# Attention without transposed probabilities: second scores with the keys on the partitions

## The chip, the core and the metric

The kernel runs on one core of a Trainium2 chip. The metric is the device time of one execution in microseconds (us), here as the median of the runs. The core has five engines with a queue each: TensorE (PE) multiplies matrices out of SBUF into PSUM, its weight loads are shown apart as PEld; VectorE (DVE) and ScalarE (ACT) work elementwise and read and write PSUM; GpSimd (POOL) works elementwise in SBUF and issues some of the DMAs; SyncE (SP) issues most DMAs. Each engine executes its queue in order.

## The reference

One layer of a hybrid diffusion backbone over 512 latent tokens and 256 context tokens, width 1024: a modulated RMS norm, one input projection, a bidirectional state-space mixer beside windowed attention, gated merge and output projection, then a gated convolutional feed-forward part. The change concerns the attention of the latent queries:

```
s_win  = q . k * scale          (latent keys within +-128, masked by -inf outside)
s_ctx  = q . k_ctx * scale      (all 256 context keys)
logits = concat(s_win, s_ctx, sink)      16 heads, 4 key heads, head size 64
p      = softmax(logits)
o      = p[window] @ v + p[context] @ v_ctx
```

Queries are taken in blocks of 128. A block sees its own, the block before and the block after (those that exist) and two context blocks: 4 or 5 key blocks of 128.

## The kernel before

All large products are done in fp32r, with each fp32 operand split into a high part (rounded by ACT) and a low part (the difference, by DVE). A product of a 128 x 128 weight block with 512 columns is three matmuls: high by high, high by low, low by high (`gemm`, L232 to L241).

The attention stage handles 16 blocks `n`: key head `j = n // 4` with its four query heads, query block `b = n % 4`. `block_atoms` (L956) lists the steps of a block as atoms: a name, an engine, a planned duration, the atoms it needs, a rank, and the function that emits it. `Plan.order` (L342) goes through them as a small planner: on each engine the atom of lowest rank that is ready next is taken, and its planned end releases others. The result is one fixed order by hand for the engines named in `manual_schedule` (L1383). Beside the blocks the plan holds products from the list `BESIDE` (L1364; `product_atoms`, L1085): the query projections of later heads, the second key projection, and gate and output projections, in pieces of three matmuls. Their matmuls have the highest rank numbers, so TensorE takes them when no attention step is ready; their weight splits (`w`, `v`) and evacuations come first on ACT and DVE.

A block before the change, with c = 4 or 5 key blocks:

- `score(i)`: per head, queries on the partitions. A query tile holds the high part in one half of the 128 rows and the low part in the other; the keys' high parts (`khi`, in both halves) and low parts (`klo`) are multiplied one after the other, into one score tile of 512 or 640 keys.
- `least(i)` on DVE adds the window mask and takes the negated maximum over keys and sink into a column of `mneg`; `exps(i)` on ACT makes the exponentials and their sum; `sink`, `sum_` and `norm(i)` divide them.
- `turn(x, i)` transposes each head's 128 x 128 probabilities of key block x by TensorE into a PSUM bank; `high(x)` and `low(x)` split the result; `values(x, y)` multiplies each part with a 128-wide stationary operand whose columns are the values' high (64) and low (64) parts. `out_low` and `out_sum` add the two halves of the result into `att`.

`q_high` and `q_low` (L899, L904) split a projected pair of query heads and place the parts in the halves of two tiles by three DMAs on SP. `k_high`, `k_low`, `k_double` do the like for the keys. `v_step` (L917) projects the values just before the stage and splits them. `split_atoms` (L1345) splits `att` for the output projection and reuses the tiles of the keys. `sum_step` (L160) issues the weight-sum DMAs of the feed-forward part on POOL, each behind one of the products' DVE splits (32 in this stage, one or two per product).

Of the kernel before, what the change touches and what calls it, by code (L numbers as in the profile page):

```python
# [44 lines left out]
def tile_hybrid_layer(  # L45
# [25 lines left out]
    win_d: bass.AP,  # L71
    fg_d: bass.AP,
# [178 lines left out]
    dtv = cpool.tile([P, 2], F32, name="dtv")  # L251
    sel = cpool.tile([P, P], U8, name="sel")
# [166 lines left out]
    winm = ap.tile([P, 896], F32, name="winm")  # L419

# [6 lines left out]
    with tc.tile_pool(name="spool", bufs=1) as sp:  # L427
# [69 lines left out]
        def load_tables():  # L497
            nc.sync.dma_start(vec[:, V_N2:], vecs[:, V_N2:])
            self_ = raws["self"] = sp.tile([P, P], F32, name="self_")
            nc.sync.dma_start(self_, sel_d)  # L500
            for d, s in ((cosb, cos_d), (sinb, sin_d), (winm, win_d), (bcs, bc.partition_broadcast(P)), (dtv, dta)):
                nc.sync.dma_start(d, s)
# [333 lines left out]
    khi = attp.tile([P, 4, 768], F32R, name="khi")  # L836
    klo = attp.tile([P, 4, 768], F32R, name="klo")

    kt = [k.rearrange("p a b -> p (a b)")[:, i * L : (i + 1) * L] for k in (khi, klo) for i in range(6)]
    atth, attl = kt[0:4] + [None] * 2 + kt[4:6], kt[6:10] + [None] * 2 + kt[10:12]  # L840
    vst = a2p.tile([P, 6, 4, P], F32R, name="vst")
# [22 lines left out]
    def k_high(r, t, z):  # L864

        S.copy(khi[:, 2 * t, z], r[:, : z.stop - z.start])

    def k_low(r, t, z):
        V.tensor_tensor(klo[:, 2 * t, z], r[:, : z.stop - z.start], raw(khi[:, 2 * t, z]), ALU.subtract)
# [10 lines left out]
    def k_step(t):  # L880
        def fn(w, r=None):
            if r is None:
                pl = accb()
                gemm([LAT(pl)], w)
                r = rope(pl, -0.125)
            pc = accb()
            gemm([CTX(pc)], w)
            rc = tmp("tc")
            S.activation(rc[:, :LC], pc[:, :LC], AF.Copy, scale=-0.125)
            for x, z in ((r, KL), (rc, KC)):  # L890
                k_high(x, t, z)
                k_low(x, t, z)
            k_double(t)

        return [("k", t)], fn
# [3 lines left out]
    def q_high(r, t):  # L899
        q = [attp.tile([P, L], F32R, tag="q", name="q", bufs=7) for _ in range(2)]  # L900
        S.copy(q[0], r)
        Q.update({2 * t: q[0], 2 * t + 1: q[1]})

    def q_low(r, t):  # L904

        q = Q[2 * t], Q[2 * t + 1]
        lo = tmp("tc").bitcast(F32R)
        V.tensor_tensor(lo, r, raw(q[0]), ALU.subtract)
        for o, i in ((q[1][64:128, :], q[0][64:128, :]), (q[1][0:64, :], lo[64:128, :]), (q[0][64:128, :], lo[0:64, :])):
            nc.sync.dma_start(raw(o), raw(i))  # L910
# [6 lines left out]
    def v_step(*w):  # L917
# [32 lines left out]
    psum_pools(acc=(2, 1), score=(1, 2), pt=(3, 1), po=(1, 1))  # L950
# [5 lines left out]
    def block_atoms(n, turned):  # L956
# [5 lines left out]
        cols = parts[0] + parts[1]  # L962
        w, c = len(cols) * P, len(cols)
        o0 = P if w == 640 else 0
        m = winm[:, 0:512] if b == 3 else winm[:, 896 - w :]
        d = {"pt": {}, "pth": {}, "ptl": {}, "p": {}, "ps": {}}
        R = 1000 * n

        def score(i):
            h = 4 * j + i  # L970
            if i == 0:
                d["mneg"] = a2p.tile([P, 4], F32, tag="mneg", name="mneg", bufs=2)
                d["den"] = a2p.tile([P, 4], F32, tag="den", name="den", bufs=2)
            ps = d["ps"][i] = bank("score")
            o = o0
            for z in parts:
                for v, k in enumerate((khi, klo)):
                    T.matmul(  # L978
                        ps[:, o : o + len(z) * P], Q[h][:, b * P : (b + 1) * P], k[:, j, z[0] * P : (z[-1] + 1) * P],
                        start=v == 0 and o % 512 in (0, P), stop=v == 1, skip_group_check=True,  # L980
                    )
                o += len(z) * P

        def least(i):
            h = 4 * j + i
            p = d["p"][i] = a2p.tile([P, 640], F32, tag="p", name="p", bufs=NP_)
            V.tensor_tensor_reduce(  # L987
                p[:, :w], d["ps"][i][:, o0 : o0 + w], m, op0=ALU.add, op1=ALU.min, scale=1.0,
# [3 lines left out]
        def exps(i):  # L992
            p = d["p"][i][:, :w]
            S.activation(p, p, AF.Exp, bias=d["mneg"][:, i : i + 1], scale=-1.0, accum_out=d["den"][:, i : i + 1])  # L994

        def sink():
            d["es"] = a2p.tile([P, 4], F32, tag="es", name="es", bufs=2)
            V.tensor_tensor(d["es"], bcs[:, 32 + 4 * j : 36 + 4 * j], d["mneg"], ALU.add)

        def sum_():  # L1000
            V.tensor_tensor(d["es"], d["es"], d["den"], ALU.add)
            V.reciprocal(d["es"], d["es"])

        def norm(i):
            p, e = d["p"][i][:, :w], d["es"][:, i : i + 1]
            if i % 2:
                S.activation(p, p, AF.Copy, scale=e)
            else:
                V.tensor_scalar(p, p, e, None, ALU.mult)

        def turn(x, i):
            if x not in d["pt"]:
                d["pt"][x] = bank("pt")
            T.transpose(d["pt"][x][:, i * P : (i + 1) * P], d["p"][i][:, x * P : (x + 1) * P], ident)  # L1014

        def high(x):
            d["pth"][x] = a2p.tile([P, L], F32R, tag="pth", name="pth", bufs=2)
            S.copy(d["pth"][x], d["pt"][x])  # L1018

        def low(x):  # L1020
            d["ptl"][x] = a2p.tile([P, L], F32R, tag="ptl", name="ptl", bufs=2)
            V.tensor_tensor(d["ptl"][x], d["pt"][x], raw(d["pth"][x]), ALU.subtract)  # L1022

        def values(x, y):
            if x == 0 and y == "pth":
                d["po"] = bank("po")
            T.matmul(  # L1027
                d["po"], vst[:, cols[x], j, :], d[y][x], start=x == 0 and y == "pth", stop=x == c - 1 and y == "ptl"
            )

        def out_low():
            d["o2"] = tmp("tc")
            S.copy(d["o2"][0:64, :], d["po"][64:128, :])

        def out_sum():
            po4 = d["po"][0:64, :].rearrange("p (t u q) -> p u t q", t=2, u=2)
            o24 = d["o2"][0:64, :].rearrange("p (t u q) -> p u t q", t=2, u=2)
            for u in range(2):
                V.tensor_tensor(
                    att[64 * u : 64 * u + 64, 2 * j : 2 * j + 2, b * P : (b + 1) * P], po4[:, u], o24[:, u], ALU.add  # L1040
                )
            if n == 3:
# [6 lines left out]
        for i in range(4):  # L1049
# [4 lines left out]
            atom("S%d.%d" % (n, i), "PE", 0.83e-3 * w + 0.055, needs, R - 600 + 10 * i, lambda i=i: score(i))  # L1054
            needs = ["S%d.%d" % (n, i)] + (["c%d" % (n - 2)] if n > 1 else [])
            if k >= NP_:
                f, g = of(k, NP_)
                needs.append("T%d.%d.%d" % (f, (3, 4, 4, 3)[f % 4], g))
            atom("r%d.%d" % (n, i), "DVE", 1.09e-3 * w + 0.195, needs, R - 600 + 10 * i, lambda i=i: least(i))
            atom("e%d.%d" % (n, i), "ACT", 0.83e-3 * w + 0.39, ["r%d.%d" % (n, i)], R - 600 + 10 * i, lambda i=i: exps(i))  # L1060
        atom("a%d" % n, "DVE", 0.16, ["r%d.3" % n], R + 50, sink)
        atom("b%d" % n, "ACT", 0.19, ["a%d" % n], R + 50, lambda: S.activation(d["es"], d["es"], AF.Exp))
        atom("c%d" % n, "DVE", 0.37, ["b%d" % n, "e%d.3" % n], R + 50, sum_)
        for i in range(4):
            e, cost = ("ACT", 0.84e-3 * w + 0.28) if i % 2 else ("DVE", 0.52e-3 * w + 0.215)
            atom("n%d.%d" % (n, i), e, cost, ["c%d" % n], R + 60 + i, lambda i=i: norm(i))
        for x in range(c):
            g, nx = len(turned), "%d.%d" % (n, x)
            turned.append(nx)
            for i in range(4):  # L1070
                needs = ["n%d.%d" % (n, i)] + (["l" + turned[g - 3]] if g > 2 else [])
                atom("T%s.%d" % (nx, i), "PE", 0.109, needs, R + 100 + 10 * x + i, lambda x=x, i=i: turn(x, i), load=0.055)
            back = turned[g - 2] if g > 3 else None
            needs = ["T%s.%d" % (nx, i) for i in range(4)]
            atom("h" + nx, "ACT", 0.587, needs + (["H" + back] if back else []), R + 100 + 10 * x, lambda x=x: high(x))
            atom("l" + nx, "DVE", 0.687, ["h" + nx] + (["L" + back] if back else []), R + 100 + 10 * x, lambda x=x: low(x))
            needs = ["h" + nx] + (["H%d.%d" % (n, x - 1)] if x else ["f%d" % (n - 1)] if n else [])
            atom("H" + nx, "PE", 0.227, needs, R + 104 + 10 * x, lambda x=x: values(x, "pth"))
# [1308 lines left out]
```

## Time and profile before

| what | value |
|---|---|
| time, median of 3 runs | 1217.41 us (1216.89 to 1217.82) |
| profiled execution: its span, first to last instruction | 1215.7 us |
| median of the runs less that span | 1.7 us |
| TensorE clock granted | 1.000 |
| attention stage: first score, last value matmul | 94.4 us, 317.4 us |
| transposes of probabilities, start of first and last | 108.5 us, 315.5 us |
| matmuls of scores, transposes, values | 256, 288, 144 |

The profile gives no other time for the profiled execution than its span; the runs that are timed have no profile. In a line of a group stand source line, engine, operation, output and inputs by the program's names, shapes, count, then busy time in us and mean duration in ns, then the engine's idle time ahead of the group and what ended it. In a line of a timeline stand start, duration, engine, line, operation. Matmuls are pipelined, so their durations overlap; the distance from one start to the next tells what a matmul takes of the stream.

### The profile page before, as it was taken

Reading aid. Unit: us, or ns where it says so; the run is one execution under the profiler, and the core shown is the slowest. Engines: PE = TensorE matmul, PEld = TensorE weight load, DVE = VectorE, ACT = ScalarE, POOL = GpSimd, SP = SyncE. Lnnn points to the kernel's source line nnn. Section 1 sums busy time; section 2 is a strip of 40 time slices with the busy share of each in tenths; the row PEclk is TensorE's granted clock in tenths of the full one; section 3 lists DMA queues with packets and bytes.
Section 4 is the critical chain, followed back from the end, with each engine's and each line's share of the span. In section 5 each row is a group of like instructions: output and inputs, shape, how many; then the busy total and the mean of one; then the engine's idle time right before and its main releaser. Section 6 shows DMA issues by size and latency. Waiting matters only on the chain.

```text
span 1215.7 us, 17471 instructions
## 1 busy us (share of the span) xinstructions
PE 1208.4 (99%) x6288; PEld 992.9 (82%) x6288; DVE 923.6 (76%) x1494; ACT 683.4 (56%) x1269; POOL 220.9 (18%) x242
## 2 busy tenths in 40 slices
PE   9999999999999999999999999999999999999998
PEld 6798888888878877778787778888988888888886
DVE  5857888888565688697896867677687777778787
ACT  5557787778544367476575664223543443436654
POOL 0000121100102534252451622000200100110021
PEclk9999999999999999999999999999999999999999
DMA  9655889834758525356366558777266634436662
GB/s 371 258 139 184 160 239 263 170 139 137 170 154 257 172 85 175 116 128 202 96 160 207 171 186 273 242 232 249 51 161 149 194 118 135 133 105 222 214 185 98
DMA packets 124424, 215.74 MB, mean 177 GB/s; under 512 B 26697, under 2 KB 69745, under 8 KB 124337
## 3 DMA queue, kind: packets, MB, share of 16 engines
q1 hardware_dynamic: 110256, 187.09, 49.1%
q0 software_dynamic: 13792, 27.27, 9.9%
q8 instruction: 49, 0.80, 0.3%
q14 instruction: 39, 0.31, 0.1%
q10 hardware_dynamic: 288, 0.27, 0.1%
HBM read 187.78 MB, written 44.89 MB: 191 GB/s over the span
## 4 chain that ended last, share of the span: by engine, by line
PE 98%; issue 1%; DVE 0%; ACT 0%; POOL 0%; DVEq 0%; POOLq 0%; ACTq 0%
PE acc L238 20%; PE acc L241 20%; PE acc L239 20%; PE score L978 3%; PE po L1027 3%; PE pt L1014 2%; PE mis L581 2%; PE mis L1707 2%; PE mis L1579 2%; PE mis L2244 2%; PE mis L2245 2%; PE mis L2243 2%; PE mis L1715 1%; PE acc L2244 1%; PE acc L2245 1%; PE acc L2243 1%
## 5 line engine op out<-in xcount | busy, mean ns | idle before, releaser
L183 ACT CAST whi<-wraw 128x1024 fp32r<-128x1024 f32 (+1 forms) x115 | 120.3, 1047 | 159.3 <-PE acc L239 104.7
L184 DVE TENSOR_TENSOR wlo<-wraw,whi 128x1024 fp32r<-128x1024 f32 (+1 forms) x115 | 144.7, 1259 | 68.2 <-ACT whi L183 65.8
L238 PE MATMUL acc<-hlh,whi 128*128 128x512 f32 x472 | 193.9, 411 | 0.0
L239 PE MATMUL acc<-hll,whi 128*128 128x512 f32 x472 | 184.9, 392 | 0.0
L241 PE MATMUL acc<-hlh,wlo 128*128 128x512 f32 x472 | 184.9, 392 | 0.0
L241 PE MATMUL acc<-mh,wlo 128*128 128x512 f32 x368 | 143.3, 389 | 0.0
L238 PE MATMUL acc<-mh,whi 128*128 128x512 f32 x368 | 143.3, 389 | 0.0
L239 PE MATMUL acc<-ml,whi 128*128 128x512 f32 x368 | 143.2, 389 | 0.0
L241 PEld LDWEIGHTS acc<-hlh,wlo 128*128 128x128 f32 x472 | 88.6, 188 | 19.5
L238 PEld LDWEIGHTS acc<-hlh,whi 128*128 128x128 f32 x472 | 88.8, 188 | 17.9 <-issue 2.8
L239 PEld LDWEIGHTS acc<-hll,whi 128*128 128x128 f32 x472 | 88.9, 188 | 17.4 <-issue 2.4
L241 PEld LDWEIGHTS acc<-mh,wlo 128*128 128x128 f32 x368 | 69.1, 188 | 14.9 <-DVE wlo L184 0.5
L239 PEld LDWEIGHTS acc<-ml,whi 128*128 128x128 f32 x368 | 69.1, 188 | 14.4
L238 PEld LDWEIGHTS acc<-mh,whi 128*128 128x128 f32 x368 | 69.1, 188 | 14.2
L987 DVE CUSTOM_DVE_ANT_0 p<-score,winm,nsink 128x512 f32<-128x512 f32 (+1 forms) x64 | 51.8, 810 | 15.3 <-PE score L978 13.8
L1412 DVE SCALAR_TENSOR_TENSOR ta<-acc,half,ta 128x511 f32<-128x511 f32 (+1 forms) x66 | 43.8, 664 | 23.2 <-ACT ta L1411 23.0
L164 POOL DMA_DIRECT2D dsum<-wdn x24 | 25.4, 1146 | 193.1 <-DVE wlo L1111 171.8
L1411 ACT ACTIVATE ta<-acc,half 128x512 f32<-128x512 f32 (+1 forms) x66 | 46.8, 710 | 24.3 <-PE acc L241 23.0
L994 ACT ACTIVATE p<-p,mneg 128x512 f32<-128x512 f32 (+1 forms) x64 | 49.7, 777 | 15.4 <-DVE mneg L987 14.8
L1022 DVE TENSOR_TENSOR ptl<-pt,pth 128x512 fp32r<-128x512 f32 x72 | 47.5, 685 | 8.7 <-ACT pth L1018 7.7
L238 PE MATMUL acc<-hch,whi 128*128 128x256 f32 x176 | 53.2, 302 | 0.0
L812 DVE SCALAR_TENSOR_TENSOR tm<-wraw,csil,tm 128x512 f32<-128x512 f32 x56 | 43.1, 770 | 12.7 <-DMA wraw<-wm 12.0
(454 smaller groups left out, 3011.1 us busy)
## 6 DMA issues: line engine op xcount, KB each, us to landing
wraw<-wup SPq DMA_DIRECT2D x44, 512.0 KB, 3.8
dsum<-wdn POOLq DMA_DIRECT2D x24, 704.0 KB, 8.7
wraw<-wm SPq DMA_DIRECT2D x32, 512.0 KB, 3.6
fb<-cs_d SPq DMA_DIRECT2D x32, 512.0 KB, 6.6
wraw<-wx SPq DMA_DIRECT2D x24, 512.0 KB, 3.6
wm<-wm SPq DMA_DIRECT2D x16, 512.0 KB, 8.3
wraw<-wz SPq DMA_DIRECT2D x16, 512.0 KB, 4.3
wraw<-wos SPq DMA_DIRECT2D x16, 512.0 KB, 4.7
```

Of the source, the lines that this page charges most:

```text
L183: F["cast"] = S.copy(hi[:, :n], r[:, :n])
L184: F["sub"] = V.tensor_tensor(lo[:, :n], r[:, :n], raw(hi[:, :n]), ALU.subtract)
L238: T.matmul(ps, wh, xh[:, k0 + k, :], start=a, stop=False)
L239: T.matmul(ps, wh, xl[:, k0 + k, :], start=False, stop=False)
L241: T.matmul(ps, wl, xh[:, k0 + k, :], start=False, stop=b)
L812: V.scalar_tensor_tensor(acc, r[:, u * 512 : u * 512 + 512], sc, acc, ALU.mult, ALU.add)
L987: V.tensor_tensor_reduce(p[:, :w], d["ps"][i][:, o0 : o0 + w], m, op0=ALU.add, op1=ALU.min, scale=1.0, scalar=nsink[:, h : h + 1], accum_o ...
L994: S.activation(p, p, AF.Exp, bias=d["mneg"][:, i : i + 1], scale=-1.0, accum_out=d["den"][:, i : i + 1])
L1022: V.tensor_tensor(d["ptl"][x], d["pt"][x], raw(d["pth"][x]), ALU.subtract)
L1411: S.activation(o[:, :n], ps[:, :n], AF.Identity, scale=hcol(base_w, stride + i), bias=hcol(base_b, i))
L1412: x = V.scalar_tensor_tensor(o[:, 1:n], ps[:, 0 : n - 1], hcol(base_w, i), o[:, 1:n], ALU.mult, ALU.add)
L2243: T.matmul(ps, h, wh, start=st, stop=False, skip_group_check=True)
```

## The change

Scores are computed twice. The first time, with queries on the partitions as before, serves the maximum alone, and only the product with the keys' tile `kboth` (high part in rows 0 to 63, low part in rows 64 to 127) by a query tile that has the high part in both halves is taken: one matmul where there were two.

The maxima of a block's four heads are transposed by TensorE to four rows (`turn_shift`), copied by ACT and put by a DMA on ACT's queue as row 64 under the queries' low parts (`row(64)`); a second row, 96, gets the exponential of sink minus maximum (`row(96)`). Row 64 of the key tile `kone` is -1.

The second scores (`turned_score`) have keys on the partitions and 4 heads x 128 queries as columns: one matmul of `kboth` by the queries' high parts, and one of 65 rows, the keys' high parts and the row of -1 by the queries' low parts and the row of maxima. The result is masked on DVE where a key block lies beside the query block, and exponentiated by ACT straight into an SBUF tile `p`. No transposes, no splits of probabilities.

The values are kept in fp32, 64 columns wide. `values(x)` is two fp32 matmuls of 256 columns, one for each pair of heads, into the lower and upper 64 partitions of the result. The denominators: POOL adds the tiles `p` and the sink's row (`add`, `add_sink`), TensorE multiplies the sum with ones (`total`), DVE takes reciprocals and multiplies (`share`, `put`). The plan now orders POOL's instructions of this stage too. The rows of the attention's output projection are reordered on the host to match the new order of heads in `att`. PSUM in this stage: two banks for products, one pair for scores, two for second scores and two for results (before: two, one pair, three for transposes, one). The scratch space for POOL's DMA descriptors is set to 4096 bytes a partition.

```diff
     def k_high(r, t, z):
-        S.copy(khi[:, 2 * t, z], r[:, : z.stop - z.start])
+        S.copy(kboth[:, 2 * t + 1, z], r[:, : z.stop - z.start])
     def k_low(r, t, z):
-        V.tensor_tensor(klo[:, 2 * t, z], ..., raw(khi[:, 2 * t, z]), ALU.subtract)
-    def k_double(t):
-        for k in (khi, klo):
-            for a in (64, 0):
-                nc.sync.dma_start(raw(k[a : a + 64, 2 * t + 1, :]), raw(k[64:128, 2 * t, :]))
-            nc.sync.dma_start(raw(k[64:128, 2 * t, :]), raw(k[0:64, 2 * t, :]))
+        V.tensor_tensor(kone[:, 2 * t + 1, z], ..., raw(kboth[:, 2 * t + 1, z]), ALU.subtract)
+    def k_place(t):
+        h = kboth[:, 2 * t + 1, :], kone[:, 2 * t + 1, :]
+        lo, hi = slice(0, 64), slice(64, P)
+        for o, i in (
+            (kboth[lo, 2 * t, :], h[0][lo]), (kone[lo, 2 * t, :], h[0][lo]), (kboth[hi, 2 * t, :], h[1][lo]),
+            (kboth[lo, 2 * t + 1, :], h[0][hi]), (kone[lo, 2 * t + 1, :], h[0][hi]), (kboth[hi, 2 * t + 1, :], h[1][hi]),
+        ):
+            nc.sync.dma_start(raw(o), raw(i))
+        G.tensor_scalar(kone[64:65, 2 * t : 2 * t + 2, :], ones..., -1.0, None, ALU.mult)
...
     def q_low(r, t):
+        j, i = divmod(2 * t, 4)
+        (b, a), lo, hi = Q[j], slice(0, 64), slice(64, P)
+        V.tensor_tensor(a[:, i, :], r, raw(b[:, i, :]), ALU.subtract)
+        for o, x in (
+            (b[lo, i + 1, :], b[hi, i, :]), (b[hi, i + 1, :], b[hi, i, :]), (a[lo, i + 1, :], a[hi, i, :]),
+            (b[hi, i, :], b[lo, i, :]),
+        ):
+            nc.sync.dma_start(raw(o), raw(x))
...
-            S.copy(vst[:, t, :, 0:64], o)
-            V.tensor_tensor(vst[:, t, :, 64:128], o, raw(vst[:, t, :, 0:64]), ALU.subtract)
+            S.copy(vst[:, t, :, :], o)
...
-    psum_pools(acc=(2, 1), score=(1, 2), pt=(3, 1), po=(1, 1))
+    psum_pools(acc=(2, 1), score=(1, 2), st=(2, 1), po=(2, 1))
...
+        cols = con + [b] + ([b + 1] if b < 3 else []) + ([b - 1] if b else [])
...
+        def turn_shift():
+            d["po"] = bank("po")
+            d["mt"] = d["po"][0:4, 256:384]
+            T.transpose(d["mt"], raw(d["mr"]), ident)
+        def row(part):
+            t = a2p.tile([4, P], F32, tag="row%d" % part, name="row", bufs=2)
+            if part == 64:
+                S.copy(t, d["mt"])
+            else:
+                S.activation(t, d["mt"], AF.Exp, bias=sink4[:, j : j + 1])
+            S.dma_start(raw(Q[j][1][part : part + 1, :, tok]), t)
+        def turned_score(x):
+            ps, k = bank("st"), slice(cols[x] * P, (cols[x] + 1) * P)
+            T.matmul(ps, kboth[:, j, k], Q[j][0][:, :, tok], start=True, stop=False)
+            T.matmul(ps, kone[0:65, j, k], Q[j][1][0:65, :, tok], start=False, stop=True)
+        def exps(x):
+            d["p"][x] = a2p.tile([P, L], F32, tag="p", name="p", bufs=NP_)
+            S.activation(d["p"][x], d["st"][x], AF.Exp, scale=-1.0)
+        def add(x):
+            ...
+                G.tensor_tensor(d["sum"], d["p"][0] if x == 1 else d["sum"], d["p"][x], ALU.add)
+        def add_sink():
+            s = h4(d["sum"])[96:97]
+            G.tensor_tensor(s, s, raw(Q[j][1][96:97, :, tok]), ALU.add)
+        def values(x):
+            for u in range(2):
+                T.matmul(
+                    d["po"][64 * u : 64 * u + 64, 0:256], vst[:, cols[x], j, :], d["p"][x][:, 256 * u : 256 * u + 256],
+                    start=x == 0, stop=x == c - 1, skip_group_check=True,
+                )
+        def total():
+            for u in range(2):
+                T.matmul(
+                    d["po"][64 * u : 64 * u + 64, 256:512], ones[:, 0:64], d["sum"][:, 256 * u : 256 * u + 256],
+                    start=False, stop=True, skip_group_check=True,
+                )
+        def share():
+            V.reciprocal(d["rec"], d["po"][:, 256:512])
+        def put():
+            V.tensor_tensor(att[:, 2 * j : 2 * j + 2, tok], x, r, ALU.mult)
...
+        atom("bt%d" % n, "PE", 0.1, ["bm%d" % n] + (["f%d" % (n - 2)] if n > 1 else []), R - 550, turn_shift, load=0.03)
+        atom("bg%d" % n, "ACT", 0.66, ["bt%d" % n], R - 550, lambda: row(64), whole=False)
+        atom("bM%d" % n, "DMA", 3.0, ["bg%d" % n], R, None)
...
+            needs = ["bM%d" % n] + ([turned[g - 2]] if g > 1 else [])
+            atom("s" + nx, "PE", 0.454, needs, R + 100 + 10 * x, lambda x=x: turned_score(x))
...
+            atom("e" + nx, "ACT", 0.62, needs, R + 100 + 10 * x, lambda x=x: exps(x))
+            needs = ["e" + nx] + (["V%d.%d" % (n, x - 1)] if x else [])
+            atom("V" + nx, "PE", 0.427, needs, R + 104 + 10 * x, lambda x=x: values(x))
...
+            atom("A" + nx, "POOL", 1.4 if x else 0.0, needs, R + 104 + 10 * x, lambda x=x: add(x))
+        atom("bz%d" % n, "POOL", 1.0, ["A%d.%d" % (n, c - 1), "bE%d" % n], R + 170, add_sink)
+        atom("bd%d" % n, "PE", 0.214, ["bz%d" % n, "V%d.%d" % (n, c - 1)], R + 180, total)
+        atom("bc%d" % n, "DVE", 1.9, ["bd%d" % n], R + 180, share)
+        atom("f%d" % n, "DVE", 0.42, ["bc%d" % n], R + 180, put)
...
-    with tc.manual_schedule(engines={mybir.EngineType.PE, mybir.EngineType.Activation, mybir.EngineType.DVE}):
+    with tc.manual_schedule(engines={mybir.EngineType.PE, mybir.EngineType.Activation, mybir.EngineType.DVE, mybir.EngineType.Pool}):
...
-    nc = bacc.Bacc("TRN2", target_bir_lowering=False, num_devices=1)
+    nc = bacc.Bacc("TRN2", target_bir_lowering=False, num_devices=1, dynamic_dma_scratch_size=4096)
```

More of the change, by code (lines that the diff above doesn't have):

```diff
@@ L990, in least @@
             )
[L992 to L1002, printed above, removed]
@@ L1020, in low @@
[L1020 to L1033, printed above, removed]
@@ L1061, in block_atoms @@
[L1061 to L1066, printed above, removed]
+            atom("S%d.%d" % (n, i), "PE", 0.42e-3 * w + 0.027, needs, R - 600 + 10 * i, lambda i=i: score(i))
@@ L1067, in block_atoms @@
+        atom("bM%d" % n, "DMA", 3.0, ["bg%d" % n], R, None)
+        atom("bi%d" % n, "ACT", 0.7, ["bg%d" % n], R - 540, lambda: row(96), whole=False)
+        atom("bE%d" % n, "DMA", 3.0, ["bi%d" % n], R, None)
         for x in range(c):
             g, nx = len(turned), "%d.%d" % (n, x)
[L1069 to L1078, printed above, removed]
@@ L1079, in block_atoms @@
[L1079 to L1083 removed]
+            turned.append("e" + nx)
+            needs = ["bM%d" % n] + ([turned[g - 2]] if g > 1 else [])
```

147 lines of the change are left out of this document (73 added, 74 removed).

## Prediction

> **What bounds the kernel now.** I read the page's head and chain of waits first, then the stretch view of the attention stage, then its instruction groups, then TensorE's timeline inside it.
>
> ```profile
> span 1215.7 us, 17471 instructions
> PE 1208.4 (99%) x6288; PEld 992.9 (82%) x6288; DVE 923.6 (76%) x1494; ACT 683.4 (56%) x1269; POOL 220.9 (18%) x242
> PE 98%; issue 1%; DVE 0%; ACT 0%; POOL 0%; DVEq 0%; POOLq 0%; ACTq 0%
> ...
> 108.00:318.00 210.00, 209.95 (x1166) 179.55 (x1165) 175.25 (x363) 168.05 (x328) 26.60 (x28) 1.00 0.71 185
> ```
>
> The last row's columns are length, then busy time of TensorE (PE), its weight loads, VectorE (DVE), ScalarE (ACT), GpSimd (POOL), then granted clock, DMA share and GB/s. TensorE sets the end and its clock is full. In the attention stage it has no idle time (209.95 of 210.00), while DVE and ACT are at 83% and 80%. "Busy" overlaps between matmuls, so I price TensorE by the distance between starts. Work taken from DVE or ACT gains nothing by itself here; a microsecond taken from or put on TensorE's stream counts in full.
>
> **What goes away.** The stage's groups:
>
> ```profile
> L987 DVE CUSTOM_DVE_ANT_0 p<-score,winm,nsink 128x512 f32<-128x512 f32 (+1 forms) x64 | 51.8, 810 | 15.3 <-PE score L978 13.8 <-PE pt L1014 1.2
> L994 ACT ACTIVATE p<-p,mneg 128x512 f32<-128x512 f32 (+1 forms) x64 | 49.7, 777 | 15.4 <-DVE mneg L987 14.8
> L1022 DVE TENSOR_TENSOR ptl<-pt,pth 128x512 fp32r<-128x512 f32 x72 | 47.5, 685 | 8.7 <-ACT pth L1018 7.7 <-PE po L1027 0.9
> L1014 PE MATMUL pt<-ident,p 128*128 128x128 f32 x288 | 41.7, 272 | 0.0
> L1018 ACT CAST pth<-pt 128x512 fp32r<-128x512 f32 x72 | 40.5, 589 | 9.2 <-PE pt L1014 5.4 <-DVE ptl L1022 2.9
> L1027 PE MATMUL po<-ptl,vst 128*128 128x512 f32 x72 | 28.6, 408 | 0.0
> L1007 ACT ACTIVATE p<-p,es 128x512 f32<-128x512 f32 (+1 forms) x32 | 23.7, 771 | 5.5 <-DVE es L1002 5.4
> L1009 DVE TENSOR_SCALAR p<-p,es 128x512 f32<-128x512 f32 (+1 forms) x32 | 15.5, 521 | 0.2
> ```
>
> and TensorE's timeline (start, duration, line):
>
> ```profile
> 150.87 0.28 PE L978 MATMUL score<-khi,q 128*128 128x256 f32 x1
> ...
> 151.35 0.39 PE L238 MATMUL acc<-hlh,whi 128*128 128x512 f32 x1
> 151.58 0.40 PE L239 MATMUL acc<-hll,whi 128*128 128x512 f32 x1
> ...
> 152.97 0.34 PE L978 MATMUL score<-khi,q 128*128 128x384 f32 x1
> ...
> 153.55 0.40 PE L238 MATMUL acc<-hlh,whi 128*128 128x512 f32 x1
> ...
> 310.23 1.47 PE L1014 MATMUL pt<-ident,p 128*128 128x128 f32 x12
> 311.46 0.47 PE L1097 MATMUL acc<-khi,whi 128*128 128x512 f32 x1
> 311.77 0.39 PE L1098 MATMUL acc<-klo,whi 128*128 128x512 f32 x1
> ```
>
> A split (fp32r) matmul of 512 columns takes 0.23 (151.35 to 151.58). One head's scores take 0.48 with 512 keys (150.87 to 151.35) and 0.58 with 640 (152.97 to 153.55). There are 32 heads of each kind: 33.9, and half of their matmuls go: -17.0. Twelve transposes take 1.23 and make the next matmul 0.08 late (0.31 instead of 0.23): 0.109 each, 288 of them: -31.4. The two value matmuls per key block, 144 in all, at 0.23: -33.1. Removed from TensorE: 81.5.
>
> **What comes.** Second scores: 2 x 72 matmuls of 512 columns at 0.23: +33.1. The second one contracts over 65 rows; I take no extra for it, since it is wider than half the array.
>
> The values become pairs of fp32 matmuls of 256 columns, each on half of the array's columns, and so do the 16 totals. The rows nearest to them are fp32 matmuls on 32 and on 64 columns elsewhere in this kernel:
>
> ```profile
> 31.70 0.39 PE L581 MATMUL mis<-ah,w0l 128*128 128x512 f32 x1
> 32.02 0.64 PE L531 MATMUL acc<-wm,csil 128*32 128x256 f32 x8
> 32.59 0.49 PE L581 MATMUL mis<-ah,w0h 128*128 128x512 f32 x1
> ...
> 481.70 1.09 PE L1715 MATMUL mis<-E,xs 128*64 128x128 f32 x16
> 482.72 0.50 PE L238 MATMUL acc<-hlh,whi 128*128 128x512 f32 x1
> 483.06 0.39 PE L239 MATMUL acc<-hll,whi 128*128 128x512 f32 x1
> ...
> 32.59 0.19 PEld L581 LDWEIGHTS mis<-ah,w0h 128*128 128x128 f32 x1 [0.41 <-issue]
> ```
>
> Eight matmuls on quarter columns are two rounds of 256 columns in 0.57; sixteen on half columns are eight rounds of 128, that is four of 256, in 1.02. So a round costs 0.225 and a run of rounds 0.12 on top. Entering costs 0.09 (31.70 to 32.02 is 0.32, not 0.23), leaving 0.11 (482.72 to 483.06). The halves do overlap, but each run pays 0.32, because the next weights aren't loaded ahead (the 0.41 idle before the load at 32.59). A pair alone costs 0.545; two behind each other 0.385 each.
>
> The Trainium skill, "TensorEngine Tiling (Array Packing)", states both sides: up to twice the speed for 64 columns (Theoretical Speedup), and that a change of tiling mode drains the engine (Key Properties). By the first alone the 88 pairs would cost 19.8 and the sum below would be -25.4; by the second, with the rows' price, it is what follows.
>
> How often do pairs stand together? With two score banks a block's first two key blocks are scored together and their exponentials end within one product piece, so I take the first two pairs as neighbours and the others as alone: c-1 runs for c key blocks, 56 runs for 72 pairs: 72 x 0.225 + 56 x 0.32 = 34.1. The totals wait for GpSimd and stand alone: 16 x 0.545 = 8.7. The transposes of the maxima stand alone: 16 x (0.109 + 0.09) = 3.2.
>
> Sum on TensorE: 33.1 + 34.1 + 8.7 + 3.2 - 81.5 = **-2.4**. Bounds: all pairs alone, 33.1 + 48.0 + 3.2 - 81.5 = +2.8; two runs per block, totals among them, 33.1 + 19.8 + 10.2 + 3.2 - 81.5 = -15.2.
>
> **The other engines.** The rows for the new work:
>
> ```profile
> L1253 DVE RECIPROCAL du<-du 128x128 f32<-128x128 f32 x3 | 2.7, 928 | 0.0
> L1147 DVE SCALAR_TENSOR_TENSOR te<-tb,acc 128x512 f32<-128x512 f32 x14 | 9.6, 684 | 4.0 <-ACT tb L1143 4.0
> L1143 ACT ACTIVATE tb<-acc 128x512 f32<-128x512 f32 x14 | 8.4, 599 | 3.7 <-PE acc L241 3.5
> L1559 POOL TENSOR_TENSOR ssq<-ssq,sq x11: 1280/1297/2009, 539.5 to 699.8; 128x512 f32<-128x512 f32 x11
> L164 POOL DMA_DIRECT2D dsum<-wdn x24 | 25.4, 1146 | 193.1 <-DVE wlo L1111 171.8 <-DVE ptl L1022 11.7 <-DVE es L1002 9.6
> L164 POOL DMA_DIRECT2D dsum<-dsum x8 | 4.3, 537 | 60.5 <-DVE wlo L1111 60.5
> ```
>
> ACT loses at least 49.7 + 40.5 + 23.7 and gains 72 exponentials at 0.6 (43) and 32 short rows with a DMA each, planned at 0.7 (22). DVE loses 47.5 + 15.5 and more, and gains 24 masks at 0.69 (16.5) and 16 reciprocals of 256 at about 1.86 (30). Both stay below their present load, so neither becomes the bound, and their gain is hidden behind TensorE.
>
> GpSimd is new on the path. A block's total waits for c-1 adds of 1.3 to 2.0 (the plan says 1.4) and the sink's add (plan 1.0). The plan sends the total as soon as the last is due. But GpSimd also issues the weight-sum DMAs, and each first waits for a DVE weight split; what stands behind in its queue, the adds, waits with it. The plan has no cost for this. The 32 issues took 29.7 us. They come in 24 groups, 21 of them during the blocks: 1.24 a group, and about 0.6 of waiting for the split (half of the split's 1.2). The part of the chain with no room, from the second add on, is about 2.5 x 1.4 + 1.0 = 4.5 us a block, 72 of 224 us (94 to 318), so 6.7 groups hit it with 1.84 each. About 0.9 is covered each time: TensorE is half a product piece late anyway (0.35), and pairs and totals that take longer than planned give the rest. TensorE then stands 6.7 x 0.94 = **+6.3**. Bounds: 0 (all groups fall in gaps) and 21 x 0.94 = +20. Behind the waiting total stand all later matmuls.
>
> The maximum row must land before the second scores; the plan allows 3.0.
>
> ```profile
> q<-tc SPq DMA_DIRECT2D x12, 128.0 KB, 4.2
> zs_d<-te SPq DMA_DIRECT2D x14, 256.0 KB, 2.0
> ```
>
> These are landings in the stage. The row is 2 KB on ACT's nearly empty queue, so I put it near 2.0: no wait. At 4.2 it would be (4.2 - 3.0 - 0.35) x 16 = +14. SP's extra copies for q (four, not three, with one wait as before) and k (two waits in a row) lie behind products that take TensorE 5.5 us each: nothing, unless the next q is late. The 128 KB mask table rides in the first loads and isn't needed until the blocks: nothing.
>
> Total: -2.4 + 6.3 = +3.9 on a span of 1215.7, so 1219.6. The median of the runs, 1217.41, lies 1.7 above the span; predicted **1221**.
>
> **Rivals.**
> *The gain arrives.* Pairs stand together more often, and GpSimd has room between adds (it was busy 26.60 of 210 us). With 40 runs in place of the 72 (56 + 16): -2.4 - 32 x 0.32 = -12.6, and some 3 of waits: -9.6, about 1208. For it: 0.9 us of unplanned cover per block; against: nothing ties pairs together in the order, which takes what is ready. This is the case on the other side; it decides if waits stay below 2 us and runs below 56.
> *Gain and waits cancel* within 0.2%: waits of 2 instead of 6, about 1217.
> *The row is late*: +14 on -2.4 and 6.3: 1235. For it: the 4.2 row; against: another queue and a 60th of the bytes.
> *The halves don't overlap* or the 65-row matmul changes the mode: 88 x 0.225 = +19.8, about 1241. Against it: the rows above.
> By the skill's speedup alone (above) the time would be 1192; the 0.41 idle speaks against it, and I count it at 0.02 inside the first rival's chance.
>
> **Chances.** The forecast 0.46, of which 0.10 lie within 0.2%; the gain arrives 0.38; cancelled 0.10; late row 0.04; no overlap 0.02. So faster by over 0.2% (2.4 us, about what a measurement of this kernel can tell from no change) 0.38, within 0.20, slower 0.42. The range reaches to TensorE's low bound (-15.2) and on the high side to waits of about 18 with all pairs alone: 1202 to 1238; the forecast's own is 1218 to 1228.
>
> **What would show it.** In the changed profile: pairs of the values 0.3 to 0.6 apart from start to next start, with the idle weight load behind each run; adds of 1.3 to 1.5 with weight-sum DMAs between them; and TensorE idle ahead of the totals, released by GpSimd, of 4 to 9 us in sum. DVE and ACT should be less busy than 175 and 168 us in a like stretch. I am wrong if TensorE doesn't wait for GpSimd (then 1215 or less), if pairs cost under 0.4 on average, or if it waits ahead of the second scores.

## The result and the profile after

The changed kernel takes **1260.23 us** (median of four runs, 1258.35 to 1260.99), the kernel before beside it 1217.32. The ratio is 1.035, 95% interval 1.0335 to 1.0365: slower by 43 us, where 1221 was forecast and 1238 was the end of the range.

The head of the page of the kernel after, and its chain of waits:

```profile
span 1256.6 us, 17374 instructions
PE 1227.8 (98%) x6240; PEld 963.3 (77%) x6240; DVE 910.7 (72%) x1376; ACT 609.4 (49%) x1109; POOL 322.8 (26%) x316
PE 87%; DMA 4%; POOL 3%; DVE 3%; issue 2%; ACT 1%; SPq 0%; ACTq 0%; DVEq 0%; POOLq 0%
```

The span is 40.9 us longer. The chain, 98% TensorE before, now has 87% of it and parts of DMA and GpSimd.

The stretch view of the kernel after, with the columns of the same view before: the attention stage with its products, and two short pieces of it.

```profile
94.00:406.00 312.00, 291.08 (x1405) 201.00 (x1404) 201.12 (x317) 125.84 (x224) 126.10 (x104) 0.97 0.61 159
192.00:196.00 4.00, 4.00 (x12) 2.79 (x13) 2.82 (x4) 0.00 (x0) 1.98 (x2) 0.53 0.67 96
256.00:260.00 4.00, 3.79 (x13) 2.88 (x14) 1.77 (x2) 0.00 (x0) 0.16 (x1) 0.65 0.91 144
```

TensorE now has 20.9 us without work in the stage, and its granted clock falls to 0.53 and 0.65 in places. DVE is busy in 201 of 312 us (64%), ACT in 126 (40%).

I add up TensorE's timeline from the stage's first score to its last product (`oa`, L1124) in three parts: idle time (in brackets in the timeline), time lost by the clock (one less the granted clock, times the time at work, in pieces of 2 us), and the rest, TensorE's own stream at full clock. The end of the last matmul ahead of a gap counts as stream, 0.16 us each time at full clock (0.39 of duration less 0.23 from start to start):

| kernel | stage | idle | lost by the clock | stream |
|---|---|---|---|---|
| before | 271.4 | 0.0 | 0.0 | 271.4 |
| after | 311.6 | 20.8 | 3.6 | 287.2 |
| difference | +40.2 | +20.8 | +3.6 | +15.8 |

**The stream.** The groups of the kernel after, shapes apart, and TensorE's timeline (start, duration, line, count):

```profile
L1048 PE MATMUL po<-p,vst 128*64 128x256 f32 x288 | 43.8, 399 | 0.0
```

```profile
168.77 0.39 PE L243 MATMUL acc<-hlh,wlo 128*128 128x512 f32 x1
169.09 0.65 PE L1048 MATMUL po<-p,vst 128*64 128x256 f32 x4
169.67 0.50 PE L1024 MATMUL st<-qboth,kboth 128*128 128x512 f32 x1
170.01 0.40 PE L1025 MATMUL st<-qlow,kone 65*128 65x512 f32 x1
...
200.10 1.08 PE L1048 MATMUL po<-p,vst 128*64 128x256 f32 x8
201.12 0.50 PE L1024 MATMUL st<-qboth,kboth 128*128 128x512 f32 x1
```

The code issues 72 x 2 = 144 value matmuls; the group has 288. One fp32 matmul stands in the trace as two instructions. A pair is "x4": from 169.09 to 169.67 it takes 0.58, with 0.09 on entry and 0.11 on leaving 0.78. Two pairs ("x8") take 1.02 and the same 0.20. So the second pair adds 0.44, the streaming of a pair, and a run costs 0.34 beside that.

**The idle time.** 14.54 of the 20.8 us stand at one place:

```profile
177.01 0.40 PE L243 MATMUL acc<-hlh,wlo 128*128 128x512 f32 x1
191.95 1.12 PE L1055 MATMUL po<-sum,ones 128*64 128x256 f32 x4 [14.54 <-POOL sum L1044]
193.70 0.63 PE L240 MATMUL acc<-hlh,whi 128*128 128x512 f32 x1
194.13 0.63 PE L241 MATMUL acc<-hll,whi 128*128 128x512 f32 x1
...
256.21 0.65 PE L1055 MATMUL po<-sum,ones 128*64 128x256 f32 x4 [2.76 <-POOL sum L1044]
```

GpSimd's timeline there:

```profile
182.45 4.08 POOL L884 TENSOR_SCALAR kone<-ones 1x1536 fp32r<-1x1536 f32 x1 [13.78 <-DMA kboth<-kone]
186.62 1.26 POOL L1040 TENSOR_TENSOR sum<-p 128x512 f32<-128x512 f32 x1
187.96 2.60 POOL L1040 TENSOR_TENSOR sum<-sum,p 128x512 f32<-128x512 f32 x2
190.64 1.26 POOL L1044 TENSOR_TENSOR sum<-sum,qlow 1x512 f32<-1x512 f32 x1
```

L884 is the end of `k_place(1)`: it writes the row of -1 into the keys' low parts and must wait until SP's DMAs have read what stands there (SP's timeline, first and last of the six):

```profile
166.94 0.47 SPq L883 DMA_DIRECT2D kboth<-kboth  x1
...
179.55 0.46 SPq L883 DMA_DIRECT2D kboth<-kone  x1
```

Behind the instruction, in GpSimd's queue, stand the adds of the block under way, and TensorE stands before that block's total. After the gap the products are 0.43 apart (193.70 to 194.13) instead of 0.23: the half clock.

Waits of the kernel after (what waited, for what, sum, times, longest):

```profile
POOL dsum L166 <- DVE wlo L1136: 83.0, 20, 8.1
PE po L1055 <- POOL sum L1044: 18.5, 4, 14.5
PE po L1012 <- DVE mr L1007: 1.9, 3, 0.8
PEld st L1025 <- DMA qlow<-row: 0.4, 1, 0.4
```

Without the 14.5, TensorE stands some 4 us for GpSimd and 1.9 for the maxima.

### The profile page after: what moved, and what is told of

Same layout as the page of the kernel before. It is cut to its first block, busy times and chain, and to the rows that moved or that the text cites. A ratio compares the mean times of both kernels' runs of the same rounds, so it can differ in the third digit from the quotient of the medians.

```text
span 1256.6 us, 17374 instructions
## 1 busy us (share of the span) xinstructions
PE 1227.8 (98%) x6240; PEld 963.3 (77%) x6240; DVE 910.7 (72%) x1376; ACT 609.4 (49%) x1109; POOL 322.8 (26%) x316
## 4 chain that ended last, share of the span: by engine, by line
PE 87%; DMA 4%; POOL 3%; DVE 3%; issue 2%; ACT 1%; SPq 0%; ACTq 0%; DVEq 0%; POOLq 0%
PE acc L240 18%; PE acc L243 17%; PE acc L241 17%; PE mis L585 2%; PE po L1048 2%; PE mis L1733 2%; PE mis L1605 2%; PE mis L2270 2%; PE mis L2269 2%; PE mis L2271 2%; POOL sum L1040 1%; PE st L1024 1%; PE mis L1741 1%; PE acc L2270 1%; PE acc L2269 1%
## 5 line engine op out<-in xcount | busy, mean ns | idle before, releaser
L1034 ACT ACTIVATE p<-st 128x512 f32<-128x512 f32 x72 | 41.8, 598 | 83.4 <-PE st L1025 63.5
L1000 DVE CUSTOM_DVE_ANT_0 score<-score,winm,nsink 128x512 f32<-128x512 f32 (+1 forms) x64 | 52.3, 816 | 30.4 <-PE score L991 30.3
L1040 POOL TENSOR_TENSOR sum<-sum,p 128x512 f32<-128x512 f32 x40 | 54.8, 1369 | 20.1 <-ACT p L1034 18.4
L1136 DVE TENSOR_TENSOR wlo<-wraw,whi 128x1024 fp32r<-128x1024 f32 x30 | 39.5, 1316 | 19.5 <-ACT whi L1133 19.4
```

Source lines behind the costliest of these rows:

```text
L1000: V.tensor_tensor_reduce(x, x, m, op0=ALU.add, op1=ALU.min, scale=1.0, scalar=nsink[:, h : h + 1], accum_out=d["mneg"][:, i : i + 1],)
L1034: S.activation(d["p"][x], d["st"][x], AF.Exp, scale=-1.0)
L1040: G.tensor_tensor(d["sum"], d["p"][0] if x == 1 else d["sum"], d["p"][x], ALU.add)
L1136: sum_step(V.tensor_tensor(d["w"][1], d["r"], raw(d["w"][0]), ALU.subtract), 1 + (4 <= g < 12))
```

## Experiments

Theory: the loss is (a) a pair's streaming of 0.44 instead of 0.225, (b) the key row in GpSimd's queue, with the half clock behind it, (c) the waits that the prediction foresaw. Rival: these gaps are interchangeable, and filling one leaves TensorE to wait for what is late next.

**The key row later.** One GpSimd instruction moves.

```
             nc.sync.dma_start(raw(o), raw(i))
+        if t == 0:
+            k_row(t)
+
+    def k_row(t):
         G.tensor_scalar(kone[64:65, ...], ..., -1.0, None, ALU.mult)
...
+            atom("kw", "DMA", 17.0, ["z" + G_], R, None)
+            atom("kr", "POOL", 4.1, ["kw"], 7e3, lambda: k_row(t))
```

> The kernel after, with one instruction moved: GpSimd's write of the row of -1 for the second pair of key heads is an atom of its own, planned 17 us after the keys' split, and the second scores of the later key heads wait for it. Theory (GpSimd stood 13.8 us for the keys' DMAs with three adds and a sink behind it, and TensorE 14.54 us for the total behind those): the 14.5 us go, and with them most of the 2 us that TensorE's half clock cost behind the long idle; the row still takes 4.1 us of GpSimd at its new place, which may hold one total for up to 2 us. 1260.2 - 14.5 - 2 + (0 to 2) = 1244 to 1246, and no wait above 4 us in front of a total. Rival (another late transfer or TensorE's own stream sets that place anyway): TensorE waits at the same place for something else; 1256 to 1260.

1248.14 us (1246.27 to 1251.11), ratio 1.0255 (1.0237 to 1.0273): 12 us less, so (b) holds, but 2 to 4 us of the expected gain are missing. The 14.5 and the half clock are gone (granted clock 1.00 throughout in the profiled execution); idle time is 10.3. GpSimd and then TensorE of this kernel:

```profile
192.33 4.09 POOL L888 TENSOR_SCALAR kone<-ones 1x1536 fp32r<-1x1536 f32 x1
196.50 3.52 POOL L1044 TENSOR_TENSOR sum<-sum,p 128x512 f32<-128x512 f32 x2
200.10 1.26 POOL L1048 TENSOR_TENSOR sum<-sum,qlow 1x512 f32<-1x512 f32 x1
```

```profile
197.94 0.39 PE L243 MATMUL acc<-hlh,wlo 128*128 128x512 f32 x1
201.42 0.65 PE L1059 MATMUL po<-sum,ones 128*64 128x256 f32 x4 [3.09 <-POOL sum L1048]
```

At its new place the row's own 4.09 us fall between two adds of a block, and that block's total is 3.09 late. The clock has a part too: two of the four executions were granted 0.999 over the whole kernel and took 1246.3 and 1246.6 us, the profiled one among them; the two others were granted 0.996 and 0.995 and took 1249.7 and 1251.1. All further runs build on this kernel.

**Pairs twice.**

```
-            for u in range(2):
+            for u in (0, 1, 0, 1):
                 T.matmul(d["po"][64 * u : 64 * u + 64, 0:256], vst[:, cols[x], j, :], ...
```

> The run with the later key row, with the two value matmuls of each key block issued twice in a row (so that the outputs are not the reference's: all values but those of a block's first key block enter twice). No switch is added. Theory (a pair of fp32 matmuls is four instructions in the trace and streams 0.45 us): 72 x 0.45 = 32 us above the run with the later row, less up to 3 us where TensorE waits anyway: 1273 to 1277. Rival (the prediction's price of 0.225 for a pair holds, and the extra time of the change comes from elsewhere): 72 x 0.225 = 16 us above it, about 1260.

1269.04 us, 20.9 above the run with the later row: between the two figures, so only the trace decides.

```profile
L1052 PE MATMUL po<-p,vst 128*64 128x256 f32 x576 | 75.0, 389 | 0.1
```

```profile
161.52 1.08 PE L1052 MATMUL po<-p,vst 128*64 128x256 f32 x8
162.54 0.50 PE L240 MATMUL acc<-hlh,whi 128*128 128x512 f32 x1
```

What was "x4" and 0.58 is "x8" and 1.02. The times from the starts of the value matmuls to the next starts, without idle time, sum to 70.9 us instead of 40.1: 30.8 for 72 pairs, **0.43 each**. The stream grows by 29.9; idle time falls from 10.3 to 2.2, as if slower values gave GpSimd time. 29.9 - 8.1 = 21.8, where the medians differ by 20.9. So (a) holds, with more of the extra work hidden in time that TensorE waited before than the 3 us I had allowed.

**Values in two runs per block.**

```
-            atom("V" + nx, "PE", 0.427, needs, ..., lambda x=x: values(x))
+            y = 1 if x < 2 else c - 1
+            if x == y:
+                xs = range(0, 2) if x == 1 else range(2, c)
+                ...
+                atom("V" + nx, "PE", 0.33 + 0.45 * len(xs), needs, ..., lambda xs=xs: [values(z) for z in xs])
```

> The run with the later key row, and the value matmuls of a block issued in two runs: key blocks 0 and 1 together, the rest together (32 runs for the 72 pairs, where about 58 were seen, totals apart). Theory (each run pays 0.32 us for going to half-array matmuls and back, whatever its length): 26 x 0.32 = 8.3 us below the run with the later row alone, about 1236. Rival (only the streaming of the pairs costs, the switch is hidden): no difference, about 1244. Third way: values issued later keep probability buffers longer and delay the exponentials: slower than 1244.

1258.65 us: 10.5 slower than the run with the later row. The runs (totals included) fall from 73 to 47 and the stream from 289.7 to 279.0, 0.41 per run saved: the switch is real. But idle time rises to 23.6 (17.2 of it for GpSimd ahead of totals), and 9.2 us go to the clock. One such place:

```profile
261.67 0.39 PE L243 MATMUL acc<-hlh,wlo 128*128 128x512 f32 x1
264.40 1.12 PE L1059 MATMUL po<-sum,ones 128*64 128x256 f32 x4 [2.34 <-POOL sum L1048]
...
266.04 0.63 PE L240 MATMUL acc<-hlh,whi 128*128 128x512 f32 x1
266.47 0.63 PE L241 MATMUL acc<-hll,whi 128*128 128x512 f32 x1
```

A gain of 10.7 in the stream was paid back twice over by waits.

**The weight sums untied.** `sum_step` gets a flag, and the stage's DMAs no longer depend on the split: first for all products, then only from the fifth on.

```
-            tc.add_manual_dep(dma.ins, ins.ins.name, BEHIND, ...)
+            if wait:
+                tc.add_manual_dep(dma.ins, ins.ins.name, BEHIND, ...)
...
-            sum_step(V.tensor_tensor(...), 1 + (4 <= g < 12))
+            sum_step(V.tensor_tensor(...), 1 + (4 <= g < 12), wait=False)      (then: wait=g < 4)
```

> The run with the later key row, and the weight-sum DMAs of the attention stage no longer tied to a split on VectorE (order and data are the same; they issue when GpSimd comes to them). Theory (each group first waits for a split, and the adds behind it in GpSimd's queue wait with it; TensorE's remaining idle ahead of totals is about 6 us): 3 to 6 us below the run with the later row alone, about 1240. Rival (the adds of 1.3 us and the issues of 1.1 us hold the totals by themselves, the wait for the split is covered): 0 to 1 us below it, about 1244.

1253.57 us, 5.4 slower. GpSimd, with nothing to wait for, issued the first sums at the kernel's very start; the DMA view up to 60 us shows their size:

```profile
1.38 2.36 POOL L166 DMA_DIRECT2D dsum<-wdn  x4
```

```profile
dsum<-wdn POOLq DMA_DIRECT2D x4, 704.0 KB, 9.6
```

The 2.9 MB run beside the first loads, which already fill the DMA engines, and the stage begins at 103.2 instead of 94.2. Inside the stage idle time fell only from 10.3 to 8.3.

> The run with the later key row, and the weight-sum DMAs untied from VectorE's splits, but only from the fifth product on, so that none issues into the loads at the kernel's start (in the run that untied all of them the attention stage began 9 us later, while inside the stage the waits ahead of totals went from 5.7 us to none, and the waits for the maxima from 2.8 to 5.4). Theory (the waits for the splits are worth what the prediction gave them): 4 to 6 us below the run with the later row (1248.1), 1242 to 1244. Rival (a released total only brings TensorE earlier to what is late next): within 1.5 us of it, 1247 to 1250.

1245.01 us, 3.1 below the run with the later row: between theory and rival. The waits of this kernel's TensorE no longer name GpSimd; the maxima have taken its place (2.8 before):

```profile
PE po L1017 <- DVE mr L1012: 5.4, 4, 2.9
```

**The total with the next block's values**, to give it slack and save its switch.

```
-        atom("bd%d" % n, "PE", 0.214, ["bz%d" % n, "V%d.%d" % (n, c - 1)], R + 180, total)
+        LAST[n] = total
...
+            if x == 0 and n:
+                needs += ["bz%d" % (n - 1)]
+                atom("V" + nx, "PE", 1.22, needs, R + 104, lambda: (LAST[n - 1](), values(0)))
```

> The run with the later key row, and the total of each block (two matmuls with ones) issued directly ahead of the next block's first pair of value matmuls, instead of as soon as GpSimd's chain of adds is planned to end (the planner is also told 0.78 us for a pair and 1.22 us for the two pairs together). Theory (TensorE's 5.7 us of waits for GpSimd ahead of totals come from a total that has no slack; and a total that shares a run with a pair of values pays no switch of its own): 5.7 + 15 x 0.32 = 10 us below the run with the later row: 1236 to 1240. Rival (as with the untied weight sums, the wait only moves to what is late next, the maxima from VectorE): only the switches are gained, about 1243.

1248.53 us, no gain. The 18 runs saved show in the stream (282.9, 6.8 less), but idle time is 16.9 and 4.5 go to the clock. TensorE's waits:

```profile
PE score L995 <- DMA qboth<-qboth: 5.3, 1, 5.3
PE score L995 <- DVE mneg L1004: 3.7, 5, 1.4
PE po L1059 <- POOL sum L1048: 3.5, 2, 2.7
```

Now a query's DMAs and the maxima are late. The theory that the waits belong to the totals falls.

> The same, with the values of a block issued in two runs (key blocks 0 and 1 behind the last block's total, then the rest). In the run with two runs alone TensorE's own stream was 10.7 us shorter at full clock, but 13 us of idle time and 9 us at half clock came in, most of it ahead of totals. Theory (with the totals out of the way the shorter stream arrives): 8 to 11 us below the run with only the later totals, 1226 to 1230. Rival (values that are issued together wait for the last of their exponentials and hold probability buffers, whatever the totals do): idle time of more than 10 us stays, 1238 or more.

1238.41 us (ratio 1.0172, 1.0155 to 1.0189), 10 below the run with only the later totals. The stream is 275.1 with 32 runs (7.8 for 23 runs, 0.34 each), idle time 13.7. It is the fastest run that keeps all of the change.

> Key row later, totals with the next block's values, values in two runs, weight-sum DMAs untied from the fifth product on: all of the change kept, with the maximum. Theory (untying removes waits wherever GpSimd's chain is what is late; without the first scores it gave 16.6 us because 15.5 us of such waits stood there, here 4.6 us do): 4 to 6 us below the run without untying (1238.4), 1232 to 1235, and still 15 us above before, because the stage's stream at full clock without idle time (275 us) is already 4 us longer than before's 271 and the other waits stay. Rival (the waits move, as with the untied sums and single pairs): within 2 us of it, 1236 to 1240.

1240.97 us: no gain. That is 2.6 above the run without untying, just outside the rival's 2 us, but the rival's mechanism is there: TensorE waits 5.7 us for GpSimd (4.6 without untying) and 3.4 for the maxima's row (0.7):

```profile
PE po L1060 <- POOL sum L1049: 5.7, 3, 3.1
PE st L1030 <- DMA qlow<-row: 3.4, 4, 1.7
```

**The values' part undone.**

```
-            atom("V" + nx, "PE", 0.427, needs, ..., lambda x=x: values(x))
+            atom("h" + nx, "ACT", 0.55, ["e" + nx] + ..., lambda x=x: high(x))
+            atom("l" + nx, "DVE", 0.6, ["h" + nx] + ..., lambda x=x: low(x))
+            atom("H" + nx, "PE", 0.227, ..., lambda x=x: values(x, "h"))
+            atom("L" + nx, "PE", 0.227, ..., lambda x=x: values(x, "l"))
```

> The run with the later key row, with the values' part of the change undone: the probabilities (with the keys on the partitions) are split into a high part by ScalarE and a low part by VectorE and multiplied as two split matmuls of 512 columns with a stationary operand of high and low values, as in the kernel before; the two halves of the result are added and then scaled. Only the 16 totals are pairs of fp32 matmuls. (Probability buffers 4 instead of 8, one buffer each for sums, reciprocals and rows; the maxima's transposes write into the totals' bank.) Theory (the column halves cost 0.43 streaming and some 0.35 of switching for each key block where two split matmuls cost 0.46; ScalarE and VectorE have room for 45 us each): the stage's stream falls by 72 x 0.3 = 17 to 22 us, 1226 to 1231. Rival (the work that returns to ScalarE and VectorE makes them late, or the fewer buffers do): idle time of TensorE above 15 us, 1236 or more.

1291.91 us. The stage's last product starts at 440.4 here. Up to there the stream falls only to 285.1, 4.6 less instead of the 17 to 22 expected, idle time is 45.2 and 15.2 go to the clock. There are 54 gaps instead of 12, and the ends of the matmuls ahead of them, counted as stream, come to some 9 us instead of 1. What the column halves cost against the split values when TensorE does not wait, this run therefore does not show. The stage up to 420, and what TensorE waits for:

```profile
94.00:420.00 326.00, 280.47 (x1173) 204.36 (x1172) 276.00 (x408) 166.11 (x296) 139.99 (x104) 0.94 0.56 144
```

```profile
PE po L1063 <- DVE ptl L1058: 14.3, 18, 1.9
PE po L1063 <- ACT pth L1054: 12.1, 16, 2.9
PE tot L1069 <- POOL sum L1050: 8.7, 6, 2.2
```

DVE is at 85% of that stretch. How much comes from its load and how much from the halved buffers this run does not tell apart.

**Without the first scores.**

```
-            atom("S%d.%d" % (n, i), "PE", ..., lambda i=i: score(i))
-            atom("r%d.%d" % (n, i), "DVE", ..., lambda i=i: least(i))
-        atom("bm%d" % n, ...)
-        atom("bt%d" % n, ...)
...
-                S.copy(t, d["mt"])
+                S.activation(t, ident[0:4, :], AF.Copy, scale=0.0, bias=-45.0)
```

> The run with later totals and two runs of values, without the first scores: the 128 score matmuls, VectorE's 64 masked minima and the transposes of the maxima are left out, and a constant of 45 takes the maximum's place in the 65th row (for other inputs that is no safe softmax). It prices what the change keeps for the maximum. Theory (TensorE sets the end, and these matmuls stand in its stream): 19 us of scores, 0.5 of transposes and some 3 of waits for the maxima go: 1238.4 - 22 = 1216, at most 2 us from before. Rival (with the scores the cover ahead of the row, the exponentials and the adds goes as well): idle time grows, 1222 or more.

> The same, with the weight-sum DMAs untied from the fifth product on. Theory (4.6 us of waits for GpSimd ahead of totals): 3 to 5 us below the run without the first scores, 1211 to 1213, and so below the kernel before. Rival (the waits move): the same as that run within 1.5 us.

1228.18 us and 1211.57 us. The first lost half of its expected gain to waits for GpSimd; the second has hardly any left:

```profile
PE po L1062 <- POOL sum L1049: 15.5, 9, 4.5
```

```profile
PE po L1063 <- POOL sum L1050: 2.3, 5, 0.9
```

The two streams are equal (248.5 each, from the first of the second scores on); untying alone gave 16.6 us here, where it gave 3 with the scores in place and nothing with all repairs. The second is faster than before (ratio 0.9957, 0.9941 to 0.9974), but it gives up the maximum, so it is no version of this kernel to use; it shows what the maximum costs in this layout: 29.4 us between the two kernels with untied sums, 10.2 between the two without.

## Why the prediction was wrong

The stage grew by 40.2 us where 3.9 were forecast. The 36.3 between them are 18.2 of TensorE's stream, 14.5 of idle time at the key row and 3.6 of clock; the other idle time, 6.3, equals the forecast's.

**TensorE's sum, -2.4 forecast, +15.8 measured.** The step that failed is "Eight matmuls on quarter columns are two rounds of 256 columns ... So a round costs 0.225". The row's x8 was four fp32 matmuls in two instructions each, one round; the x16 of the half columns was eight matmuls, two rounds of 256 and not four. The code beside the row, counted, would have shown it: L531 runs 64 times and L1715 128 times, and the groups of the kernel before have twice as many:

```profile
L1715 PE MATMUL mis<-E,xs 128*64 128x128 f32 x256 | 17.5, 279 | 0.0
L531 PE MATMUL acc<-wm,csil 128*32 128x256 f32 x128 | 9.4, 400 | 0.0
```

The price is 0.43 to 0.45: 88 x 0.22 = 19 us too little, where -2.4 and +15.8 lie 18.2 apart, so the other terms together came out about 1 us lower than forecast. The bound "all pairs alone" (+2.8) rested on the same 0.225, so the true value lay outside both bounds. The excess is about that of my rival in which the halves don't overlap (+19.8), but that is chance, for the rows speak for overlap: four matmuls on quarter columns stream 0.45 (the prediction's 0.57 less 0.12), two on half columns 0.44. Matmuls of 256 columns one behind the other would take twice as long for four as for two. Fp32 matmuls on all columns stand beside the half columns in the kernel after:

```profile
480.30 1.88 PE L1733 MATMUL mis<-st,CT 128*128 128x512 f32 x4
482.12 1.09 PE L1741 MATMUL mis<-E,xs 128*64 128x128 f32 x16
```

The x4 are two matmuls of 512 columns. They take 1.82, with some 0.1 of it for entering the half columns, so 256 columns take 0.43: one matmul on all columns streams as long as a pair on halves. The sign that the prediction named, pairs 0.3 to 0.6 from start to next start, came true at 0.58 and still did not tell the prices apart: by the forecast's price it would have been 0.225 + 0.12 = 0.345.

**The switch, right.** 0.32 forecast; 0.34 to 0.41 per run of value matmuls saved in three experiments. The Trainium skill, "TensorEngine Tiling (Array Packing)", Key Properties, has a change of mode drain the engine. The trace agrees in that each change costs time, 0.09 on entry and 0.11 on leaving. The 65-row second scores stood 0.23 to 0.24 from the next start wherever no half columns came next, as taken. For 72 pairs and 16 totals I had 72 runs, and the trace has 72.

**The waits, right in kind, and in size partly by luck.** The +6.3 was for totals that wait for GpSimd. There, beside the 14.5 at the key row, 4.0 stand, at the low end of the 4 to 9 that the prediction named and inside the bounds (0 to 20); the 1.9 ahead of the maxima, for which it had no term, make up the sum. With the sums untied the waits for GpSimd went from 5.7 to nothing and the time fell by 3.1, so the weight sums do hold totals up. What I had not seen: taking such waits away mostly moves them, to maxima, rows or a query's DMAs. Idle time was 8 to 17 us in every repair that kept the first scores and the column halves (23.6 in one).

**The key row, missed.** "SP's extra copies for q ... and k ... lie behind products ... nothing" looked at SP's queue and left out that `k_place` ends in a GpSimd instruction. This is the second step that failed: a term put at nothing cost 14.5 us of idle time, and moving it gave 12. The count that was needed: 4.1 us of its own, six DMAs in a chain ahead of it, and three adds and a sink behind it.

**The clock, missed.** 3.6 us here, 9 and 15 in the runs with most waits. A wait of TensorE can cost more than its length.

**VectorE and ScalarE, right that their relief gains nothing**: they are down to 64% and 40% of the stage, and the time rose. The row was in time (one weight load, PEld, stood 0.4 us for it), so that rival falls for this kernel; with all repairs it did wait, 3.4.

## What to carry over

Before a row of a group becomes a price, divide its count by the number of calls in the code: an fp32 matmul counts twice here, a transpose once (288 of 288 in the kernel before). When a chain of work goes onto an engine's queue, list everything else that enters this queue during it, single instructions behind DMAs included, with the work that stands behind each. And where a planner writes the order, a gain in TensorE's stream arrives only if the other engines keep pace: 10.7 us of saved stream came out as a loss of 10.5.

## What the runs showed of the hardware

- GpSimd's write of the key row, one partition with 1536 elements, takes 4.1 us. An add takes 1.26 with 128 x 512 elements (L1040) and 1.26 with 1 x 512 (L1044): one partition costs as much as 128.
- The granted clock fell to half after idle gaps of 2.34 and 2.76 us, but not after one of 3.09 (201.42 in the run with the later row). The Trainium skill, "TensorE: Matmul & The Clock Gate", What's actually happening, gives half clock after at least one idle window of about 3.4 us, with windows that run freely; the 14.5 us gap agrees, the two short ones fall below that figure. What decides for gaps of 2 to 3 us stays open. Executions of one kernel differ in it: the one with the later row was granted 0.999 twice, 0.996 and 0.995.
- With untied DMAs of 2.9 MB at the kernel's start, the stage that had begun at 94.2 us began 9 us later. The bytes take 8.6 us at the 336 GB/s of the first 60 us, an estimate. From 2 to 40 us TensorE was busy for 32.5 us instead of 37.9 and its granted clock was 0.91 instead of 1.00, so part of the 9 us is clock.
